# A transformer block with 32 experts: TensorE's order in the expert stage written out, with one pair's combination inside the next pair's products and weight pieces of 8 KB rows

## The chip, the cores and the metric

The kernel runs on one core of a Trainium2 chip. The metric is the time of one execution on the device in microseconds (us). The core has five engines that run their own instruction streams: TensorE (PE, matrix products), VectorE (DVE), ScalarE (ACT), GpSimd (POOL) and SyncE (SP, which here only issues transfers). [...]

## The reference

Two blocks over 512 tokens of width 1024, all in f32. The first: attention and a Fourier mix, then a mixture of 32 experts. The second: an S5 layer, an SSD layer, an MLP behind each. The change lies in the experts and what feeds them:

```python
def hier_moe(h, w_rg, b_rg, w_re, b_re, w_gate, w_up, w_down):
    ...                                   # each token: 2 of 32 experts, and a gate for each
    h_pad = jnp.concatenate([h, jnp.zeros((1, d), h.dtype)], axis=0)
    def expert_block(args):
        tok, wt, e = args
        xb = h_pad[tok]
        y = (jax.nn.silu(xb @ w_gate[e]) * (xb @ w_up[e])) @ w_down[e]
        return y * wt[:, None]
    ...
    return out[:t]                        # the sum of a token's two results

xl = xl + gt2 * hier_moe(h2l.reshape(b * s, d), *moe_args).reshape(b, s, d)
```

`w_gate` and `w_up` are 1024x512 for each expert, `w_down` is 512x1024: 6.3 MB for an expert, 201 MB for all 32.

## The kernel before

`moe` (L916 to L1023) goes over the experts in 8 steps (`st`) of 4 experts, and each step in 2 pairs (`pr`), 16 pairs in all. A pair does, in the order of the code:

- **G, U** (L970): the gate and up products of the two experts, 32 matmuls each, 64 columns of the array for either expert, over 8 pieces of weights. `part` (L922) loads a piece of 1 MiB, 512 rows of one expert, each partition taking 4 rows of 2 KB from four places. Row `k*128 + p` of the weights stands in partition p, so `gather` reads 128 neighbouring columns of `h2h`, `h2l` for its k.
- **gather** (`pg`, L910, L911): for the 4 experts of the next step, the tokens' vectors are picked by products with a one-hot matrix `oh`, 64 matmuls in four PSUM tiles; ScalarE copies them to `xg` (L914). The code has it in each second pair (`pr == 1`) alone.
- **phT** (L982): silu on ScalarE (`sg`), times U on VectorE, then four transposes to `hT`. **pw** (L988): the gate of each slot, eight passes of the array in f32.
- **Y** (L1001): the down product, 32 matmuls over 4 pieces, first all of the left half of the columns, then the right. VectorE scales it (`y`, L1005), ScalarE and VectorE split it into a high and a low part (`yh`, `yl`, L1006, L1007).
- **S5 tables**: `next(self.blocks)` runs one block of `s5_blocks` (L1496 to L1556), which prepares tables of the second block: two transposes `pcd` (L1518), eight VectorE operations on `pb` and `m3` (L1526 to L1538), four transposes `pm2` (L1543), products `pkt` (L1550, L1551), copies `Cd`, `me`, `kt` on ScalarE and three transfers on GpSimd's queue. They use the one PSUM buffer of `psz`.
- **combination**: `pohT` (L1012) transposes the one-hot matrix, and 16 products `pcmb` (L1019, L1020) add the pair's results to the tokens, 8 additions on VectorE (`x`, L1022).

PSUM gives this stage seven buffers, taken in turn by all of these. Nothing orders TensorE's instructions but data, buffers and the scheduler's own choice, so the code's order isn't the order on the engine: in most steps the gather and `pohT` stand inside the products of U and Y. Weights go through a ring of eight buffers of 1 MiB and two of their own (`own`); SP issues a load when TensorE has used up what lay in the buffer.

Ahead of the stage, `pre` computes the tokens' normalised vectors `h2h` (ScalarE, L615) and their remainder `h2l` (VectorE, L620), and in between `router` its choice, with two small operations on ScalarE (L875, L881).

Of the kernel before, what the change touches and what calls it, by code (L numbers as in the profile page):

```python
# [98 lines left out]
class Build:  # L99
    def __init__(self, tc, a, out, ctx, taps=None, mode="all"):  # L100
        self.tc, self.nc, self.a, self.out, self.taps, self.mode = tc, tc.nc, a, out, taps or {}, mode
        self.ctx = ctx
        self.overflow, self.split_eng = True, None
        self.g = self.pool(ctx, "glob", 1)
        self.big = self.pool(ctx, "big", 5)
        self.psz = self.pool(ctx, "psz", 1, space=PSUM)
        self.dr = ctx.enter_context(tc.tile_pool(name="dr", bufs=1, space=DRAM))
# [26 lines left out]
    def split(self, w, shape, pool, name="w", eng=None):  # L134
# [6 lines left out]
        return h, l  # L141

# [245 lines left out]
    def pre(self):  # L388
# [136 lines left out]
        next(self.blocks)  # L525
# [26 lines left out]
        self.sc2, self.sh2 = sc2, sh2  # L552
        nc.vector.scalar_tensor_tensor(sc2, sc2, 1.0, self.col["g_ffn"], op0=ADD, op1=MUL)
        wr, wrs = [late[:, i, 0:288].rearrange("p (k n) -> p k n", k=8) for i in (1, 2)]
# [58 lines left out]

        for t in range(4):
            nc.scalar.activation(self.h2h[:, t], x1[:, t], AF.Copy, scale=rs[:, t:t + 1])  # L615
        with tc.issue_after(self.marks.ins):
            for c in range(2):
                cs = slice(c * 512, c * 512 + 512)
                for t in range(4):
                    nc.vector.scalar_tensor_tensor(self.h2l[:, t, cs], x1[:, t, cs], rs[:, t:t + 1], self.h2h[:, t, cs].bitcast(F32),  # L620
                                                   op0=MUL, op1=SUB)
# [278 lines left out]
    def gather(self, xg, oh2d, n, ks=(0, 8)):  # L900
# [3 lines left out]
        for k0 in range(*ks, per):  # L904
            pt = self.psum((128, per, n), name="pg")
            for i in range(per):
                k = k0 + i
                ks = slice(k * 128, k * 128 + 128)
                for t in range(4):
                    nc.tensor.matmul(pt[:, i], self.h2h[:, t, ks], oh2d[:, t], start=(t == 0), stop=False)  # L910
                    nc.tensor.matmul(pt[:, i], self.h2l[:, t, ks], oh2d[:, t], start=False, stop=(t == 3))  # L911
# [4 lines left out]
    def moe(self):  # L916
# [5 lines left out]
        def part(wt, e, kh, q=None):  # L922
            return self.raw(wt[e, kh * 512:(kh + 1) * 512].rearrange("(k p) n -> p k n", p=128), (128, 4, 512), q=q)
# [6 lines left out]
        down = lambda e, hf: wd[e, :, hf * 512:(hf + 1) * 512].rearrange("(k p) n -> p k n", p=128)  # L930
        xg2 = self.B((128, 2, 2048), name="xg")
        place = lambda w: w.rearrange("p (k n) -> p k n", k=4)

        def part_d(e, hf, w=None):
            if w is None:
                return self.raw(down(e, hf), (128, 4, 512))
# [7 lines left out]
        if self.overflow:  # L944
            self.moe_overflow(xg2[:, 0].rearrange("p (k n) -> p k n", k=4))
        with ExitStack() as cx:
            mp = self.pool(cx, "moe", 2)
            def prepare(st):
# [3 lines left out]

            nxt = prepare(0)
            for st in range(8):
# [4 lines left out]
                for pr in range(2):  # L959
                    eA = e0 + 2 * pr  # L960
                    so = pr * 128
                    G, U = self.psum(name="G"), self.psum(name="U")
                    for w, pt in ((wg, G), (wu, U)):
                        for kh in range(2):
# [3 lines left out]
                            for k in range(4):  # L968
                                for i in range(2):
                                    nc.tensor.matmul(pt[64 * i:64 * i + 64], xg[:, kh * 4 + k, so + 64 * i:so + 64 * i + 64],  # L970
                                                     ws[i][:, k], start=(kh == 0 and k == 0), stop=(kh == 1 and k == 3),
                                                     tile_position=(0, 64 * i), skip_group_check=True)
                    for i in range(4):
                        if pr == 1 and st < 7:
                            self.gather(nxt[1], nxt[0], 256, (2 * i, 2 * i + 2))
                    sg = mp.tile([128, 512], F32, tag="sg", name="sg")
                    hm = sg
                    nc.scalar.activation(sg, G, AF.Silu)
                    nc.vector.tensor_tensor(hm, sg, U, op=MUL)  # L979
                    pt = self.psum(name="phT")  # L980
                    for k in range(4):
                        nc.tensor.transpose(pt[:, k * 128:(k + 1) * 128], hm[:, k * 128:(k + 1) * 128], self.ident)  # L982
                    hT = mp.tile([128, 4, 128], F32, tag="hT", name="hT", bufs=1)
                    nc.scalar.activation(hT, pt.rearrange("p (k s) -> p k s", k=4), AF.Copy)

                    pw = self.psum((128, 4), name="pw")
                    for t in range(4):
                        nc.tensor.matmul(pw, oh2[:, t, so:so + 128].bitcast(F32), self.gw[:, t, e0:e0 + 4],  # L988
                                         start=(t == 0), stop=(t == 3))
                    wv = mp.tile([128, 1], F32, tag="wv", name="wv")  # L990
                    for i in range(2):
                        nc.vector.tensor_copy(wv[64 * i:64 * i + 64], pw[64 * i:64 * i + 64, 2 * pr + i:2 * pr + i + 1])
                    yh = mp.tile([128, 2, 512], F32R, tag="yh", name="yh", bufs=1)
                    yl = mp.tile([128, 2, 512], F32R, tag="yl", name="yl", bufs=1)
                    for hf in range(2):
                        ws = [ahead.pop((id(wd), hf, i)) if eA == 0 and (id(wd), hf, i) in ahead else
                              part_d(eA + i, hf, None if hf else own[i]) for i in range(2)]
                        pt = self.psum(name="Y")
                        for k in range(4):
                            for i in range(2):  # L1000
                                ip = nc.tensor.matmul(pt[64 * i:64 * i + 64], hT[:, k, 64 * i:64 * i + 64], ws[i][:, k],  # L1001
                                                      start=(k == 0), stop=(k == 3), tile_position=(0, 64 * i),
                                                      skip_group_check=True)
                        y = mp.tile([128, 512], F32, tag="y", name="y", bufs=1)
                        nc.vector.scalar_tensor_tensor(y, pt, wv, self.gt2[:, hf * 512:(hf + 1) * 512], op0=MUL, op1=MUL)  # L1005
# [4 lines left out]
                    pt = self.psum(name="pohT")  # L1010
                    for t in range(4):
                        nc.tensor.transpose(pt[:, t * 128:(t + 1) * 128], oh2[:, t, so:so + 128].bitcast(F32), self.ident)  # L1012
                    ohT = mp.tile([128, 512], F32R, tag="ohT", name="ohT", bufs=1)
                    nc.scalar.activation(ohT, pt, AF.Copy)
                    for t in range(4):
                        for hf in range(2):
                            pt = self.psum(name="pcmb")
                            ls = ohT[:, t * 128:(t + 1) * 128]
                            nc.tensor.matmul(pt, ls, yh[:, hf], start=True, stop=False)  # L1019
                            nc.tensor.matmul(pt, ls, yl[:, hf], start=False, stop=True)  # L1020
                            xs = x1[:, t, hf * 512:(hf + 1) * 512]
                            nc.vector.tensor_tensor(xs, xs, pt, op=ADD)  # L1022
# [1020 lines left out]
```

## Time and profile before

| what | us |
|---|---|
| median of 3 runs (2452.0 to 2458.82) | 2454.11 |
| the profiled execution | 2456.05 |
| its span, first to last instruction | 2454.3 |
| expert stage, first gather to last addition | 445.59 to 1063 |
| busy in the span: TensorE | 2281.1 |
| VectorE | 1353.9 |
| ScalarE | 816.7 |

[...] Two warnings for reading: a matmul's duration in a row is longer than the time between two of them, since they overlap, so a pace is read from the starts of two rows; and a TensorE that is shown busy may still be emptying one kind of product before it begins another.

### The profile page before, as it was taken

The page shows a single profiled execution, that of the slowest core. Times are in us where ns is not written, and L with a number is a line of the kernel's source. Part 1 is how long each engine was busy: PE and PEld are TensorE (multiplying, and loading weights), DVE is VectorE, ACT ScalarE, POOL GpSimd, SP SyncE. Part 2 cuts the span into 40 slices and gives each one's busy share as a digit, 9 for nine tenths or more (in the row PEclk, how much of TensorE's full clock was granted, in tenths as well). Part 3 has the DMA queues.
Part 4 walks back from the last instruction along what each step waited for, and adds up shares of the span by engine and source line. Part 5 has one row for each costly group of instructions (what it writes and reads, how often), then busy time and mean ns, then how long its engine had stood idle before and what let it go on. Part 6 is the DMA issues. An engine that isn't in the chain of part 4 may idle for free.

```text
span 2454.3 us, 32253 instructions
## 1 busy us (share of the span) xinstructions
PE 2281.1 (93%) x12503; PEld 1633.9 (67%) x12503; DVE 1353.9 (55%) x2583; ACT 816.7 (33%) x1317; POOL 240.2 (10%) x407
## 2 busy tenths in 40 slices
PE   7988999699998999979999999999999998999997
PEld 4664569344444444368788778787778777888787
DVE  4754445424334242466667884466786778544454
ACT  4232343211111111154333332335654434322332
POOL 0166000011111010000000000000221210000000
PEclk9899999899999999989999999999999999999999
DMA  8577645699999999945545772342332322233330
GB/s 282 163 219 235 196 141 189 248 326 341 355 377 322 331 331 355 340 132 160 175 125 169 228 229 91 95 123 62 112 104 87 111 78 86 69 95 95 94 96 35
DMA packets 327775, 454.02 MB, mean 185 GB/s; under 512 B 22308, under 2 KB 201252, under 8 KB 327620
## 3 DMA queue, kind: packets, MB, share of 16 engines
q1 hardware_dynamic: 318272, 435.23, 53.8%
q0 software_dynamic: 8592, 16.27, 2.1%
q8 instruction: 100, 1.64, 0.3%
q10 hardware_dynamic: 756, 0.43, 0.1%
q14 instruction: 55, 0.45, 0.1%
HBM read 436.14 MB, written 15.73 MB: 184 GB/s over the span
## 4 chain that ended last, share of the span: by engine, by line
PE 54%; DVE 8%; DMA 3%; ACT 3%; issue 2%; POOL 0%; SPq 0%; DVEq 0%; ACTq 0%; POOLq 0%
PE pt L146 13%; PE pt L147 13%; PE pt L148 13%; PE G L970 3%; PE Y L1001 3%; PE U L970 3%; DMA adaw<-in_ada_w 3%; DVE adaacc L314 1%; DVE wl L140 1%; PE pg L910 1%; PE pg L911 1%; PE py L1925 1%; PE pY L1668 0%; DVE x L1327 0%; PE pG L1637 0%
## 5 line engine op out<-in xcount | busy, mean ns | idle before, releaser
L140 DVE TENSOR_TENSOR wl<-w,wh 128x1024 fp32r<-128x1024 f32 (+2 forms) x239 | 287.4, 1207 | 225.1 <-ACT wh L139 221.0
L139 ACT ACTIVATE wh<-w 128x1024 fp32r<-128x1024 f32 (+1 forms) x241 | 249.0, 1040 | 480.5 <-PE pt L147 375.1
L146 PE MATMUL pt<-hh,wh 128*128 128x512 f32 (+2 forms) x976 | 369.0, 383 | 3.2 <-ACT hh L1219 3.0
L147 PE MATMUL pt<-hl,wh 128*128 128x512 f32 (+2 forms) x976 | 367.9, 380 | 0.1
L148 PE MATMUL pt<-hh,wl 128*128 128x512 f32 (+2 forms) x976 | 365.9, 378 | 0.0
L146 PE MATMUL pt<-ab,wh 128*128 128x512 f32 (+1 forms) x576 | 213.4, 375 | 4.8 <-ACT o L1347 2.9
L147 PE MATMUL pt<-ab,wh 128*128 128x512 f32 (+1 forms) x576 | 214.4, 373 | 1.1 <-DVE ab L1296 0.9
L148 PE MATMUL pt<-ab,wl 128*128 128x512 f32 (+1 forms) x576 | 213.7, 372 | 0.0
L146 PEld LDWEIGHTS pt<-hh,wh 128*128 128x128 f32 (+1 forms) x976 | 181.9, 188 | 44.9 <-ACT hh L1219 4.2
L147 PEld LDWEIGHTS pt<-hl,wh 128*128 128x128 f32 (+1 forms) x976 | 182.9, 188 | 39.3 <-issue 3.6
L148 PEld LDWEIGHTS pt<-hh,wl 128*128 128x128 f32 (+1 forms) x976 | 183.0, 188 | 39.0 <-issue 3.5
L1327 DVE SCALAR_TENSOR_TENSOR x<-pt,mod,x 128x512 f32<-128x512 f32 (+1 forms) x184 | 122.3, 678 | 115.2 <-PE pt L148 114.5
L970 PE MATMUL G<-w,xg 128*64 128x512 f32 x512 | 131.8, 602 | 5.3 <-DVE x L1022 5.3
L979 DVE TENSOR_TENSOR sg<-sg,U 128x512 f32<-128x512 f32 x16 | 11.0, 688 | 227.6 <-PE U L970 227.6
L970 PE MATMUL U<-w,xg 128*64 128x512 f32 x512 | 131.1, 594 | 0.0
L146 PEld LDWEIGHTS pt<-ab,wh 128*128 128x128 f32 x576 | 108.2, 190 | 30.2 <-ACT ab L1295 7.6
L147 PEld LDWEIGHTS pt<-ab,wh 128*128 128x128 f32 x576 | 109.4, 190 | 23.3 <-DVE ab L1296 3.5
L148 PEld LDWEIGHTS pt<-ab,wl 128*128 128x128 f32 x576 | 109.3, 190 | 19.9
L1914 POOL TENSOR_TENSOR ec<-ec,BC 128x384 f32<-128x384 f32 x32 | 39.9, 1263 | 686.7 <-PE pt L148 571.3
L970 PEld LDWEIGHTS G<-w,xg 128*64 128x64 f32 x512 | 38.0, 137 | 75.9 <-issue 63.0
L970 PEld LDWEIGHTS U<-w,xg 128*64 128x64 f32 x512 | 40.8, 137 | 70.7 <-issue 69.2
L1022 DVE TENSOR_TENSOR x<-x,pcmb 128x512 f32<-128x512 f32 x128 | 80.5, 673 | 4.7 <-PE pcmb L1020 4.7
(575 smaller groups left out, 4236.5 us busy)
## 6 DMA issues: line engine op xcount, KB each, us to landing
w<-in_w_gate SPq DMA_DIRECT2D x64, 1024.0 KB
w<-in_mlp_w SPq DMA_DIRECT2D x128, 512.0 KB
w<-in_w_up SPq DMA_DIRECT2D x63, 1024.0 KB
extra<-in_w_down SPq DMA_DIRECT2D x32, 1024.0 KB
w<-in_w_down SPq DMA_DIRECT2D x31, 1024.0 KB
adaw<-in_ada_w SPq DMA_DIRECT2D x48, 512.0 KB
adaw<-in_ada_w SPq DMA_DIRECT2D x96, 256.0 KB
w<-in_m_w_in SPq DMA_DIRECT2D x40, 512.0 KB
```

The costliest lines, as they stand in the source:

```text
L139: nc.scalar.activation(h, w, AF.Copy)
L140: (eng or nc.vector).tensor_tensor(l, w, h.bitcast(F32), op=SUB)
L146: nc.tensor.matmul(out, ah, bh, start=start, stop=False, skip_group_check=True)
L147: nc.tensor.matmul(out, ah, bl, start=False, stop=False, skip_group_check=True)
L148: return nc.tensor.matmul(out, al, bh, start=False, stop=stop, skip_group_check=True)
L314: nc.vector.scalar_tensor_tensor(acc, w, ck, acc, op0=MUL, op1=ADD)
L910: nc.tensor.matmul(pt[:, i], self.h2h[:, t, ks], oh2d[:, t], start=(t == 0), stop=False)
L970: nc.tensor.matmul(pt[64 * i:64 * i + 64], xg[:, kh * 4 + k, so + 64 * i:so + 64 * i + 64], ws[i][:, k], start=(kh == 0 and k == 0), stop= ...
L1001: ip = nc.tensor.matmul(pt[64 * i:64 * i + 64], hT[:, k, 64 * i:64 * i + 64], ws[i][:, k], start=(k == 0), stop=(k == 3), tile_position=(0 ...
L1022: nc.vector.tensor_tensor(xs, xs, pt, op=ADD)
L1327: self.nc.vector.scalar_tensor_tensor(xs, src, gate, xs, op0=MUL, op1=ADD)
L1914: nc.gpsimd.tensor_tensor(ec, ec, BC[:, 1, 128:512], op=MUL)
```

## The change

- `pin` chains each TensorE instruction of the stage behind the one before it in the code, so the code's order is the engine's.
- A generator `combine` holds a pair's 16 combination products. The next pair takes a quarter of them after each half of G and of U.
- PSUM's buffers have three tags: two for small things ("a"), three for G, U, Y ("gu"), two for the combination ("c").
- `pohT` comes right behind U, the gather is spread over both pairs of a step (half of a pair's share before `phT`, half behind it), `pw` becomes four products of rounded operands behind the first half of G.
- `s5_blocks` yields three times a block: the loads; `pcd` and the VectorE tables (run at a pair's end); `pm2`, `pkt`, the copies and stores (run before Y of the next pair).
- A weight piece still has 1 MiB, but a partition takes 8 KB in a row: row `p*8 + k` of gate and up, `p*4 + k` of down. So `h2h` and `h2l` are written by k, from every eighth column of `x1`; `hm` reads every fourth column of `sg` and U; and the scale and shift columns take a trip through DRAM (`ssd`, `ssp`). Y goes over both halves of its columns with the first two rows, then with the last two.
- Three tiles that nobody uses (`shift`, `shift2`, `shift3`) move the addresses of others: the big tiles by 96 bytes.

```diff
+    def pin(self, i):
+        if self.pinned:
+            if self.line is not True:
+                self.tc.add_manual_dep(i.ins, self.line.ins.name, mybir.DependencyInfo(
+                    mybir.DependencyClass.NoSync, mybir.DependencyReason.DATA), reason="pin")
+            self.line = i
+        return i
...
+        ssd = self.dr.tile([16, 128], F32, name="ssd")
+        nc.sync.dma_start(ssd, rows)
+        ssp = self.g.tile([128, 2, 8], F32, name="ssp")
+        nc.sync.dma_start(ssp, ssd.rearrange("(c r) (q k) -> (r q) c k", c=2, k=8))
...
-            nc.scalar.activation(self.h2h[:, t], x1[:, t], AF.Copy, scale=rs[:, t:t + 1])
+            nc.scalar.activation(by_k(self.h2h, t, slice(0, 8)), xk(t, slice(0, 8)), AF.Copy, scale=rs[:, t:t + 1])
...
-            return self.raw(wt[e, kh * 512:(kh + 1) * 512].rearrange("(k p) n -> p k n", p=128), (128, 4, 512), q=q)
+            return self.raw(wt[e].rearrange("(p k) n -> p k n", k=8)[:, 4 * kh:4 * kh + 4], (128, 4, 512), q=q)
...
-        down = lambda e, hf: wd[e, :, hf * 512:(hf + 1) * 512].rearrange("(k p) n -> p k n", p=128)
+        down = lambda e, kh: wd[e].rearrange("(p k) n -> p k n", k=4)[:, 2 * kh:2 * kh + 2]
...
+            def combine(ohT, yh, yl):
+                for t in range(4):
+                    for hf in range(2):
+                        pt = self.ps.tile([128, 512], F32, tag="c", name="pcmb")
+                        ls = ohT[:, t * 128:(t + 1) * 128]
+                        pin(nc.tensor.matmul(pt, ls, yh[:, hf], start=True, stop=False))
+                        pin(nc.tensor.matmul(pt, ls, yl[:, hf], start=False, stop=True))
+                        xs = x1[:, t, hf * 512:(hf + 1) * 512]
+                        nc.vector.tensor_tensor(xs, xs, pt, op=ADD)
+                        yield
...
+                    quarters = [(nxt[1], nxt[0], 256, (k, k + 2)) for k in range(0, 8, 2)] if st < 7 else []
+                    quarters = quarters[2 * pr:2 * pr + 2] if st else quarters[:4 * pr]
+                    G, U = gu("G"), gu("U")
...
+                            for _ in range(2):
+                                next(back, None)
...
+                    half = len(quarters) // 2
+                    for q in quarters[:half]:
+                        self.gather(*q)
                     pt = self.psum(name="phT")
...
+                    for q in quarters[half:]:
+                        self.gather(*q)
+                    if eA:
+                        for _ in range(2):
+                            next(self.blocks, None)
...
-                    with tc.issue_after(ia.ins), tc.issue_after(iv.ins), tc.issue_after(ip.ins):
+                    with tc.issue_after(ia.ins), tc.issue_after(iv.ins):
                         next(self.blocks, None)
...
+                    back = combine(ohT, yh, yl)
```

TensorE at the end of a pair without gather, before: the S5 block's `pcd`, the transposed one-hot matrix, the combination, with `pm2` ahead of its last product and `pkt` among the next pair's G.

```order
L1518 MATMUL pcd_4962<-cst_66,cr_4956 64x64 [waits DMASW2_49]
L1012 MATMUL pohT_5000<-cst_66,oh_4333 128x128 x4
L1019 MATMUL pcmb_5007<-yh_4917,ohT_5005 128x512 [waits Activation_49]
L1020 MATMUL pcmb_5007<-yl_4918,ohT_5005 128x512 [waits DVE_49]
...
L1543 MATMUL pm2_4982<-cst_66,pb_4973 128x128 [waits DVE_49,Activation_49]
L1543 MATMUL pm2_4982<-cst_66,pb_4973 128x128 x3
L1019 MATMUL pcmb_5035<-yh_4917,ohT_5005 128x512 [waits DVE_49]
L1020 MATMUL pcmb_5035<-yl_4918,ohT_5005 128x512
L970 MATMUL G_5039<-w_5041,xg_4097 64x512 [waits DMAHW1_49,DVE_49]
L1550 MATMUL pkt_4990<-m3_4974,pb_4973 16x128 [waits DVE_49,Activation_49]
L1550 MATMUL pkt_4990<-m3_4974,pb_4973 16x128 x3
L1551 MATMUL pkt_4990<-dd_4959,cst_66 16x4x16 [waits DMASW1_49]
```

The same engine and place now: Y ends, `pcd` follows, and the next pair's G begins at once.

```order
L1071 MATMUL Y_5222<-w_5235,hT_5169 64x512
L1589 MATMUL pcd_5254<-cst_67,cr_5214 64x64 [waits DMASW3_49,Activation_49]
L1589 MATMUL pcd_5254<-cst_67,cr_5214 64x64 [waits DMASW4_49]
L1022 MATMUL G_5275<-w_5277,xg_4117 64x512 [waits DMAHW7_49]
...
L986 MATMUL pcmb_5289<-yh_5219,ohT_5143 128x512 [waits Activation_49]
L987 MATMUL pcmb_5289<-yl_5220,ohT_5143 128x512 [waits DVE_49]
L986 MATMUL pcmb_5293<-yh_5219,ohT_5143 128x512 [waits Activation_49]
L987 MATMUL pcmb_5293<-yl_5220,ohT_5143 128x512 [waits DVE_49]
L1032 MATMUL pw_5297<-gw2_4355,oh_4813 128x8 x4
L1022 MATMUL G_5275<-w_5305,xg_4117 64x512 [waits DMAHW1_49]
```

The combination has left the pair's end, and its first quarter stands between the halves of the next G, with `pw` behind it. Second place, TensorE between U and Y of a pair, now (15 further `pg` rows behind either row of `pg`):

```order
L987 MATMUL pcmb_5130<-yl_4991,ohT_4914 128x512
L1045 MATMUL pohT_5138<-ident_r_4353,oh_4358 128x128 x4
L933 MATMUL pg_5145<-oh_4813,h2h_4005 128x256 [waits PE_49]
...
L1054 MATMUL phT_5164<-cst_67,hm_5135 128x128 [waits DVE_49,Activation_49]
L1054 MATMUL phT_5164<-cst_67,hm_5135 128x128 x3
L933 MATMUL pg_5171<-oh_4813,h2h_4005 128x256 [waits Activation_49]
...
L1615 MATMUL pm2_5191<-cst_67,pb_5036 128x128 x4
L1622 MATMUL pkt_5199<-m3_5037,pb_5036 16x128 [waits Activation_49]
L1622 MATMUL pkt_5199<-m3_5037,pb_5036 16x128 x3
L1624 MATMUL pkt_5199<-dd_4988,cst_67 16x4x16 [waits DMASW1_49]
L1071 MATMUL Y_5221<-extra_4004,hT_5169 64x512 [waits DMAHW3_49]
```

Here `pohT`, half of the gather, `pm2` and `pkt` have come to stand between U and Y. ScalarE there, now:

```order
L1048 ACTIVATE ohT_5143<-pohT_5138 128x512 [waits PE_49]
L937 ACTIVATE xg_4117<-pg_5145,ssp_3693 128x256 [waits PE_49]
L937 ACTIVATE xg_4117<-pg_5145,ssp_3693 128x256
L1056 ACTIVATE hT_5169<-phT_5164 128x512 [waits DVE_49,PE_49]
L937 ACTIVATE xg_4117<-pg_5171,ssp_3693 128x256 [waits PE_49]
L937 ACTIVATE xg_4117<-pg_5171,ssp_3693 128x256
L1616 ACTIVATE me_5190<-pm2_5191 128x512 [waits DMASW2_49,PE_49]
L1626 ACTIVATE kt_5197<-pkt_5199 16x4x128 [waits DMASW4_49,PE_49]
L1078 ACTIVATE yh_5219<-y_5245 128x512 [waits DVE_49]
```

The copy `me`, which frees the PSUM buffer for `pkt`, now stands behind two copies of the gather.

## Rows read from the trace of the kernel before

**Rows 1.** Busy time by stretch: us of it, each engine, granted clock, DMA share, GB/s.
```profile
602.74:640.00 37.26, 34.13 (x158) 14.23 (x160) 15.59 (x30) 4.55 (x9) 7.07 (x12) 0.95 1.04 361
640.00:1062.90 422.90, 388.20 (x1890) 182.06 (x1890) 149.27 (x284) 72.94 (x142) 54.42 (x89) 0.99 0.94 334
```
**Rows 2.** Waits of TensorE in the expert stage: us in total, times, longest.
```profile
PE pm L1543 <- DVE pb L1538: 14.6, 15, 1.2
PE pcmb L1019 <- ACT ohT L1014: 11.0, 16, 0.7
PE pg L910 <- DVE oh L897: 9.0, 1, 9.0
PE phT L982 <- DVE sg L979: 8.1, 9, 1.2
```
**Rows 3.** TensorE's timeline, pairs' first G: start, us, line and operation, wait.
```profile
486.64 1.70 PE L970 MATMUL G<-w,xg 128*64 128x512 f32 x2 [0.53 <-DVE x L1022]
...
1027.78 1.08 PE L970 MATMUL G<-w,xg 128*64 128x512 f32 x4
```
**Rows 4.** TensorE's timeline in one pair without gather, and Y of a later one.
```profile
529.79 1.05 PE L1550 MATMUL pkt<-m,pb 128*16 128x128 f32 x8
...
545.78 0.66 PE L982 MATMUL phT<-cst,sg 128*128 128x128 f32 x4 [0.85 <-DVE sg L979]
546.27 0.95 PE L988 MATMUL pw<-gw,oh 128*128 128x4 f32 x8
547.18 3.65 PE L1001 MATMUL Y<-extra,hT 128*64 128x512 f32 x16
550.66 3.60 PE L1001 MATMUL Y<-w,hT 128*64 128x512 f32 x16
...
558.71 0.39 PE L1019 MATMUL pcmb<-yh,ohT 128*128 128x512 f32 x1
558.93 0.39 PE L1020 MATMUL pcmb<-yl,ohT 128*128 128x512 f32 x1
...
773.62 5.35 PE L1001 MATMUL Y<-extra,hT 128*64 128x512 f32 x16
```
**Rows 5.** TensorE's timeline where weight products lie between gather products.
```profile
451.27 3.65 PE L970 MATMUL G<-w,xg 128*64 128x512 f32 x16
...
455.08 0.28 PE L911 MATMUL pg<-oh,h2l 128*128 128x256 f32 x1
455.20 0.28 PE L910 MATMUL pg<-oh,h2h 128*128 128x256 f32 x1
...
880.66 3.65 PE L970 MATMUL U<-w,xg 128*64 128x512 f32 x14
...
884.46 0.28 PE L910 MATMUL pg<-oh,h2h 128*128 128x256 f32 x1
```
**Rows 6.** ScalarE's copies of the gather, by line: busy us, mean ns, idle before.
```profile
L914 ACT ACTIVATE xg<-pg,mcol 128x256 f32<-128x256 f32 x64 | 32.6, 559 | 96.3 <-PE pg L911 96.3
```
**Rows 7.** Transfers: two stretches (columns as in Rows 1), and SP's queue, 430 to 1075.
```profile
500.00:515.00 15.00, 14.63 (x102) 10.74 (x100) 1.00 (x3) 4.56 (x9) 0.00 (x0) 1.00 1.05 386
4.00:5.50 1.50, 0.00 (x0) 0.00 (x0) 0.00 (x0) 0.00 (x0) 0.00 (x0) 1.00 1.05 420
...
q1 hardware_dynamic: 103361, 200.10, 87.7%
```
**Rows 8.** Ahead of the stage: the timeline, and a line that reads every eighth column.
```profile
430.01 2.19 ACT L615 ACTIVATE h2h<-x,rqy 128x1024 fp32r<-128x1024 f32 x2 [2.61 <-DVE rqy L212]
...
434.71 0.20 ACT L881 ACTIVATE r_ex<-r_ex 128x4 f32<-128x4 f32 x1 [0.34 <-DVE r_ex L880]
...
438.56 4.05 DVE L620 SCALAR_TENSOR_TENSOR h2l<-x,rqy,h2h 128x512 fp32r<-128x512 f32 x6
...
L1207 ACT ACTIVATE hh<-t x8: 1122/1165/1258, 1075.4 to 1089.0; 128x512 fp32r<-128x512 f32 x8
L1208 DVE TENSOR_TENSOR hl<-t,hh x8: 1099/1138/1182, 1076.5 to 1090.2; 128x512 fp32r<-128x512 f32 x8
```

More of the change, by code (lines that the diff above doesn't have):

```diff
@@ L524, in pre @@
         self.ada_ctx.close()
-        next(self.blocks)
+        for _ in range(4):
+            next(self.blocks)
         late = self.B((128, 4, D), name="late")
@@ new lines, in moe @@
+                            for _ in range(2):
+                                next(back, None)
+                            if (w is wg) and kh == 0:
+                                pw = self.psum((128, 2, 4), name="pw")
+                                for t in range(4):
+                                    pin(nc.tensor.matmul(pw, oh2[:, t, so:so + 128], gw2[:, t, st], start=(t == 0), stop=(t == 3)))
+                                wv = mp.tile([128, 1], F32, tag="wv", name="wv", bufs=4)
+                                for i in range(2):
+                                    ps = slice(64 * i, 64 * i + 64)
+                                    nc.vector.tensor_reduce(wv[ps], pw[ps, :, 2 * pr + i], axis=AX.X, op=ADD)
@@ new lines, in moe @@
+                    sg = mp.tile([128, 512], F32, tag="sg", name="sg", bufs=1)
+                    hm = mp.tile([128, 4, 128], F32, tag="y", name="hm")
+                    k4 = lambda ap: ap.rearrange("s (p k) -> s k p", k=4)
+                    nc.scalar.activation(sg, G, AF.Silu)
+                    nc.vector.tensor_tensor(hm, k4(sg), k4(U), op=MUL)
+                    pt = self.psum(name="pohT")
+                    for t in range(4):
+                        pin(nc.tensor.matmul(pt[:, t * 128:(t + 1) * 128], oh2[:, t, so:so + 128], ident_r, start=True,
+                                             stop=True, skip_group_check=True))
@@ L984, in moe @@
+                    hT = mp.tile([128, 4, 128], F32, tag="sg", name="hT", bufs=1)
                     nc.scalar.activation(hT, pt.rearrange("p (k s) -> p k s", k=4), AF.Copy)
[L986 to L990, printed above, removed]
@@ new lines, in moe @@
+                    Y = [gu("Y") for _ in range(2)]
+                    for kh in range(2):
+                        ws = [ahead.pop((id(wd), kh, i)) if eA == 0 and (id(wd), kh, i) in ahead else
+                              part_d(eA + i, kh, None if kh else own[i]) for i in range(2)]
+                        for hf in range(2):
+                            for k in range(2):
+                                for i in range(2):
+                                    pin(nc.tensor.matmul(Y[hf][64 * i:64 * i + 64], hT[:, 2 * kh + k, 64 * i:64 * i + 64],
+                                                         ws[i][:, k, hf * 512:(hf + 1) * 512], start=(kh == 0 and k == 0),
+                                                         stop=(kh == 1 and k == 1), tile_position=(0, 64 * i),
+                                                         skip_group_check=True))
@@ L1023, in moe @@
+            for _ in back:
+                pass
+            self.line = self.pinned = None
         self.tap("x2pre", x1)
```

125 lines of the change are left out of this document (64 added, 61 removed).

## The prediction

> **What bounds the kernel now.** I read the busy time by stretch first, then TensorE's waits in the expert stage, then its timeline pair by pair, then the transfers. The stage runs from 445.6 to 1063.0, 617.4 us. From the first G of the second pair to that of the last [rows 3] there are 14 pairs in 1027.78 - 486.64 = 541.1 us, so 38.65 us a pair; the first takes 41.0 and the last with its additions 35.2. What a pair's work should take I build from paces. Sixteen weight products go in 550.66 - 547.18 = 3.48 us, so the 96 of a pair in 20.9. The 16 combination products go one in 0.22 [rows 4]: 3.6. Gather products go one in 0.12 [rows 5]; 32 for each pair on average: 3.8. Four transposes take 0.49, `pohT` and `phT` 1.0; `pw` 0.9; `pm2` like the transposes 0.5; `pkt` 1.2 [rows 4]; `pcd` 0.2. That is 32.1 us of the 38.65.
>
> The rest is two things. TensorE stood idle for 422.9 - 388.2 = 34.7 us in the 10.9 pairs from 640 on [rows 1], 3.2 a pair, and the waits name who it waited for: `pm2` for VectorE's table `pb` 15 times, the combination for ScalarE's copy `ohT` 16 times, `phT` for VectorE's product 9 times [rows 2]. The other 3.3 us are shown as busy. Part of them is the change from one kind of product to another: after 16 weight products a second gather product starts 455.08 - 451.27 = 3.81 us after the first of them, of which the products and one gather product explain 3.60; in a later place 14 weight products with one gather product should take 3.17, and took 884.46 - 880.66 = 3.80 [rows 5]. The scheduler mixes gather and weight products piecemeal, so this price is paid often. Part may be weights that come late: one half of Y took 5.2 us from 773.62 on, for 3.48 [rows 4].
>
> Transfers are near their limit but not at it: their share is 0.94 from 640 on, at 334 GB/s, where a saturated stretch shows 1.05 and 386 [rows 1, 7]. A pair moves 334 x 422.9 / 10.94 = 12.9 MB.
>
> **The change, part by part.**
>
> *A pair with gather, in the fixed order.* Weights 20.9, combination 3.6, gather 3.8 (now 32 in each pair), transposes 1.0, `pw` with four passes in place of eight 0.5, `pm2`, `pkt`, `pcd` 1.9: 31.7. Changes of kind: out of G's halves, U's halves and Y, five. The low price is 0.2 on the way out, and I take 0.3 with the way back in; the high one is 0.7 (0.63 by the later place). G's whole half of 16 is the form that the new order has, so 0.3: 1.5 a pair, at most 3.5.
>
> *Waits that stay.* After `pohT` and 16 gather products TensorE does `phT`, then the other 16. With two PSUM buffers of that tag these need the buffer of the first ones, that is both copies `xg` at 0.56 each [rows 6] with some 0.2 for signals, less `phT`'s 0.49: 0.9. Then `pm2` 0.5, and `pkt` needs its one buffer back: `me` stands behind two more `xg` on ScalarE, so 2 x 0.56 + 0.6 + 0.2 - 0.5 = 1.4. Queued behind `pkt` on TensorE is Y, so both are on the path: 2.3.
>
> *Waits that go.* `pb` is made a pair ahead, so `pm2` no longer waits. `ohT` is copied while the gather runs. `phT` has 0.5 + 1.9 us of cover after U for `hm`, which now reads every fourth column; a line on VectorE that reads every eighth takes 1.14 against some 0.7 [rows 8], so it fits with a microsecond to spare. The first combination waits for `yl` of the last pair behind 3.5 us of G; `y`, `yh`, `yl` of the right half are three operations of 512 columns, on VectorE some 0.7 each (`h2l`'s six in 4.05 [rows 8]), with signals about 2.6. An addition frees a combination buffer in 0.7 and has 3.5 until the next quarter. If that cover failed it would cost some 0.5 us a pair.
>
> *Sum of a pair:* 31.7 + 1.5 + 2.3 = 35.5. Twelve pairs are of this kind: 426. The pair with the first gather, worked in the same way, 34.8 (no combination to do, but a whole gather at its start, a part of it at a low clock, and `phT` with less cover); the second has a whole gather of 64, 39.3; the last two have none, 30.7 each. At the end the combination of the last pair is left, set by VectorE's eight additions, 8.2 from Y's end. Together 569.7 for 617.4: **-47.7 us**.
>
> *The layout of 8 KB rows.* `h2h` goes from 1.1 us an operation to about 2.15, by the line that reads every eighth column (1.165 for 512) [rows 8]. `r_ex` of the router stands behind all four on ScalarE and had 0.34 to spare: +3.9. `h2l` follows on VectorE, eight operations that go from 0.74 to 1.14: +3.2. The one-hot matrix and the first gather stand behind, and TensorE idles there (9.0 us for `oh` now [rows 2]): **+7.1 us**, at least 3 if the strided read on this source costs half of that.
>
> *What it gives:* no row shows 8 KB pieces. 2 KB ones (200.10 MB in 103361 packets [rows 7]) saturate at 386, and a stretch where rows of 4 KB come in shows 420 [rows 7]. 12.9 MB take 35.7 us at the 361 of the busiest stage stretch [rows 1], 33.4 at 386, 30.7 at 420. I take 386 or better, so transfers stay behind TensorE's 35.5, except in the last two pairs. From below: nothing bars 8 KB rows from being slower than 2 KB ones, and that is a rival.
>
> *Edits at nothing:* the two small transfers `ssd`, `ssp` stand on SP between loads for the output projection, when TensorE has products loaded for several us; if their cover is gone, +2. The pads move addresses and change no instruction; no row tells a price; I take 0 and allow 6 us either way.
>
> **Sum.** Against the profiled execution 2456.05 - 47.7 + 7.1 = 2415.4. That run was 1.9 above the median of those shown, so 2413.5: **2414 us**.
>
> **Rivals.**
>
> *Changes of kind stay dear.* At 0.7 in place of 0.3, with five a pair, +2.0 us a pair, +30: 2444. For it: the later place in [rows 5], and that TensorE's busy time holds 3.3 us a pair beyond its work. Against: there 14 products stood split, and now the halves are whole.
>
> *Waits and changes hidden.* If the buffers are freed sooner than I count and a change costs what a neighbouring product hides, a pair takes 33.7, and the stage falls by 28 more: 2386. For it: half of the waits is my own sum of signals.
>
> *Transfers set the pace.* At 345 GB/s a pair takes 12.9 / 0.345 = 37.4 us, 16 pairs 598, with 8 for the end and 7 ahead 613: 2450; at 361, 2424. For it: the late Y [rows 4], and loads that wait in SP's queue for a buffer that the end of Y frees. Against: the 386. [...]
>
> *Slower than before:* one mechanism. If 8 KB rows, now 128 in a piece in place of 512, keep fewer of the 16 transfer engines busy at a time, the rate falls. From 12.9 MB in 38.1 us, 339 GB/s, the gain is gone; at 320 a pair takes 40.3, and the time is 2456 + 16 x 40.3 + 8 + 7 - 617 = 2499.
>
> *It doesn't do what it says.* If the missing 3.3 us a pair are late weights and not changes of kind, a fixed order leaves them, pairs stay near 38.5 and the strided reads add 7: about 2460.
>
> **How the numbers follow.** Forecast (with its neighbourhood 2400 to 2428) 0.50; changes dear 0.14; waits hidden 0.14; transfers 0.10; slower 0.06; no gain 0.06. A difference of 0.3%, 7.4 us, is about what a measurement of this kernel can tell from none. Faster by more: the first three and nearly all of the fourth, 0.86; slower by more: 0.08, with a part of the last; the same 0.06. The range takes in the dear changes and the hidden waits: 2386 to 2444.
>
> **What would show it.** In the changed kernel's trace: 35 to 36 us from one pair's first G to the next with gather; waits of `pkt` for `me`, about 1.4, and of the second half of the gather for `xg`, about 0.9, and none of `pm2` for `pb` or the combination for `ohT`; the first gather at about 452.7; a transfer rate above 360 with a share below 1. Pairs of 37.5 with TensorE shown busy would speak for dear changes, with a share of 1.05 for transfers. Pairs at 38.6, or a rate under 340, would make the forecast wrong.

## The result

The changed kernel takes 2384.80 us (median of 4 runs, 2384.53 to 2389.99), against 2453.06 for the kernel before beside it: a ratio of 0.9729, with a 95% interval of 0.9699 to 0.9759. That is 68 us less. The forecast was 2414, 40 us less; the measured time lies 1.2 us below the low end of the range. (Taken by the ratio from the 2454.11 of before that the forecast started from, it is 2387.6, just inside.)

The spans of the two profiled executions differ by 2454.3 - 2383.1 = 71.2 us. Three stretches share that:

| stretch | before | after | difference | forecast |
|---|---|---|---|---|
| start to the first gather of the experts | 445.6 | 451.5 | +5.9 | +7.1 |
| first gather to last addition | 617.4 | 562.9 | -54.5 | -47.7 |
| from there to the end | 1391.3 | 1368.7 | -22.6 | 0, within 6 |

So the stage came out 7 us better than forecast, and three quarters of the miss lie in a stretch to which the prediction gave nothing.

The first stretch also holds work that is nearly the same in every kernel of this case and varies by itself: the first operation on `h2h` starts between 426 and 443 us in the fourteen traces. From that operation to the first gather it is 15.6 us before and 22.4 after, 6.9 more.

### The profile after

The busy time by stretch (us of the stretch, then each engine with its number of instructions, granted clock, DMA share, GB/s), to hold against [rows 1]:

```profile
490.00:700.00 210.00, 198.93 (x1048) 98.12 (x1046) 82.54 (x152) 39.31 (x78) 34.45 (x58) 1.00 0.95 371
700.00:920.00 220.00, 208.97 (x1083) 99.86 (x1080) 94.81 (x178) 41.13 (x83) 39.02 (x66) 1.00 0.96 377
```

TensorE is idle for 430 - 407.9 = 22.1 us in 12.3 pairs, 1.8 a pair, where it was 3.2. The transfers have the same share as before and move a tenth more. TensorE's waits in the stage, to hold against [rows 2]:

```profile
PE pkt L1622 <- ACT me L1616: 16.6, 15, 1.2
PE pg L933 <- DVE oh L920: 12.4, 1, 12.4
PE pg L933 <- ACT xg L937: 8.8, 13, 0.7
PE Y L1071 <- ACT hT L1056: 0.7, 1, 0.7
PE phT L1054 <- DVE hm L1041: 0.7, 1, 0.7
```

`pm2` no longer waits for `pb`, nor the combination for `ohT` or `yh`. The two waits that the prediction said would stay are there, at 1.1 and 0.7 us a pair (forecast 1.4 and 0.9). One pair on TensorE, from the timeline (start, duration, what), to hold against [rows 4]:

```profile
640.62 3.65 PE L1022 MATMUL U<-w,xg 128*64 128x512 f32 x16
644.21 0.50 PE L986 MATMUL pcmb<-yh,ohT 128*128 128x512 f32 x1
644.54 0.39 PE L987 MATMUL pcmb<-yl,ohT 128*128 128x512 f32 x1
...
645.33 3.65 PE L1022 MATMUL U<-w,xg 128*64 128x512 f32 x16
...
655.60 0.60 PE L1615 MATMUL pm<-cst,pb 128*128 128x128 f32 x4
657.36 1.05 PE L1622 MATMUL pkt<-m,pb 128*16 128x128 f32 x8 [1.16 <-ACT me L1616]
...
658.55 3.65 PE L1071 MATMUL Y<-extra,hT 128*64 128x512 f32 x16
662.03 3.60 PE L1071 MATMUL Y<-w,hT 128*64 128x512 f32 x16
665.57 0.30 PE L1589 MATMUL pcd<-cst,cr 64*64 64x64 f32 x2
665.79 3.65 PE L1022 MATMUL G<-w,xg 128*64 128x512 f32 x16
```

Weight products come in whole halves of 16, and Y, `pcd` and the next G stand close together. In the trace the first G of one pair follows that of the last in 34.93 to 35.3 us in the twelve pairs with half of a step's gather (35.5 forecast); before, the 14 pairs of [rows 3] varied from 33.4 to 43.8.

Ahead of the stage, ScalarE and then VectorE, to hold against [rows 8]:

```profile
429.04 4.16 ACT L638 ACTIVATE h2h<-x,rqy 128x1024 fp32r<-128x1024 f32 x2 [2.62 <-DVE rqy L223]
...
437.26 0.20 ACT L904 ACTIVATE r_ex<-r_ex 128x4 f32<-128x4 f32 x1
...
441.85 6.32 DVE L643 SCALAR_TENSOR_TENSOR h2l<-x,rqy,h2h 128x512 fp32r<-128x512 f32 x6
```

`h2h` takes 2.08 us an operation for 1.1, `h2l` 1.05 for 0.68.

And one thing nobody had asked about. In the MLP of the second block, whose code the change doesn't touch, products of 512 columns follow each other like this before:

```profile
2260.16 0.40 PE L146 MATMUL pt<-hh,wh 128*128 128x512 f32 x1
2260.40 0.39 PE L147 MATMUL pt<-hl,wh 128*128 128x512 f32 x1
2260.63 0.40 PE L148 MATMUL pt<-hh,wl 128*128 128x512 f32 x1
2260.86 0.40 PE L146 MATMUL pt<-hh,wh 128*128 128x512 f32 x1
```

and after:

```profile
2192.02 0.39 PE L157 MATMUL pt<-hh,wh 128*128 128x512 f32 x1
2192.25 0.39 PE L158 MATMUL pt<-hl,wh 128*128 128x512 f32 x1
2192.47 0.39 PE L159 MATMUL pt<-hh,wl 128*128 128x512 f32 x1
2192.70 0.39 PE L157 MATMUL pt<-hh,wh 128*128 128x512 f32 x1
```

Three products take 0.70 us before and 0.68 after; the median spacing over all of them is 0.234 and 0.227 us, at the same granted clock of 1.00.

### The profile page after: what moved, and what is told of

It reads as the page before. It is cut to its first block, busy times and chain, and to the rows that moved or that the text cites. A ratio compares the mean times of both kernels' runs of the same rounds, so it can differ in the third digit from the quotient of the medians.

```text
span 2383.1 us, 32055 instructions
## 1 busy us (share of the span) xinstructions
PE 2226.4 (93%) x12440; PEld 1620.5 (68%) x12440; DVE 1362.5 (57%) x2584; ACT 820.9 (34%) x1320; POOL 237.4 (10%) x407
## 4 chain that ended last, share of the span: by engine, by line
PE 62%; DVE 8%; ACT 4%; DMA 3%; issue 3%; POOL 0%; SPq 0%; DVEq 0%; ACTq 0%; POOLq 0%
PE pt L157 12%; PE pt L158 12%; PE pt L159 12%; PE U L1022 5%; PE Y L1071 5%; PE G L1022 5%; DMA adaw<-in_ada_w 2%; PE pcmb L986 2%; PE pg L933 2%; PE pg L934 1%; PE pcmb L987 1%; DVE adaacc L325 1%; DVE wl L142 1%; ACT wh L141 1%; PE pkt L1622 1%
## 5 line engine op out<-in xcount | busy, mean ns | idle before, releaser
L157 PE MATMUL pt<-hh,wh 128*128 128x512 f32 (+2 forms) x976 | 363.4, 377 | 3.2 <-ACT hh L1289 3.0
L158 PE MATMUL pt<-hl,wh 128*128 128x512 f32 (+2 forms) x976 | 362.4, 374 | 0.0
L159 PE MATMUL pt<-hh,wl 128*128 128x512 f32 (+2 forms) x976 | 360.8, 373 | 0.0
L1022 PE MATMUL G<-w,xg 128*64 128x512 f32 x512 | 116.9, 598 | 0.0
L1022 PE MATMUL U<-w,xg 128*64 128x512 f32 x512 | 116.6, 598 | 0.0
L933 PE MATMUL pg<-oh,h2h 128*128 128x256 f32 x256 | 66.0, 295 | 21.2 <-DVE oh L920 12.4
L1022 PEld LDWEIGHTS U<-w,xg 128*64 128x64 f32 x512 | 34.1, 136 | 66.9 <-issue 62.2
```

The source lines that it names most:

```text
L157: nc.tensor.matmul(out, ah, bh, start=start, stop=False, skip_group_check=True)
L158: nc.tensor.matmul(out, ah, bl, start=False, stop=False, skip_group_check=True)
L159: return nc.tensor.matmul(out, al, bh, start=False, stop=stop, skip_group_check=True)
L933: self.pin(nc.tensor.matmul(pt[:, i], self.h2h[:, t, ks], oh2d[:, t], start=(t == 0), stop=False))
L1022: pin(nc.tensor.matmul(pt[64 * i:64 * i + 64], xg[:, kh * 4 + k, so + 64 * i:so + 64 * i + 64], ws[i][:, k], start=(kh == 0 and k == 0), s ...
```

## The experiments

Theories: the order on TensorE sets the stage's pace (the prediction's); rivals: the 8 KB rows set it, or buffers and early tables do and the fixed order little. For the later stages: the unused tiles change the products' pace by their addresses, or something else does.

### The pads

Undone in the changed kernel:

```diff
-        self.g.tile([128, 8], F32, name="shift")
-            self.tp.tile([128, 56], F32, name="shift2", bufs=1)
-        pool.tile([128, 40], F32, name="shift3", bufs=1)
```

> The changed kernel without its three unused tiles. The big tiles then start at 64 modulo 128 bytes, where the changed kernel has 96 and the kernel before 0; the f32 weight halves of the MLPs stay at 96. Theory A (the start of a product's moving operand modulo 64 bytes sets its pace: 0 is slow, 32 is fast): the later stages' products go back from 0.227 us to 0.234, about 2700 of them, +20 us: 2405. Theory B (the operand has to lie at the weights' offset modulo 128): the same here, 2405. Theory C (addresses do nothing, the later stages are faster for another reason): 2385.

Measured: 2401.10 us, ratio 0.9776 (0.9742 to 0.9809), against 0.9729 with the pads: about 12 us, though the two intervals overlap a little. The traces are clearer: up to the end of the stage the two stay within 2 us of each other, then the one without pads loses 15. Behind the stage all ten traces with the pads take 1365 to 1373 us, and this one 1384.

```profile
2204.61 0.40 PE L156 MATMUL pt<-hh,wh 128*128 128x512 f32 x1
2204.84 0.40 PE L157 MATMUL pt<-hl,wh 128*128 128x512 f32 x1
2205.08 0.40 PE L158 MATMUL pt<-hh,wl 128*128 128x512 f32 x1
2205.31 0.40 PE L156 MATMUL pt<-hh,wh 128*128 128x512 f32 x1
```

The spacing is back at 0.233. Alone in the kernel before:

```diff
+        self.g.tile([128, 40], F32, name="shift")
```

> The kernel before with one unused tile of 160 bytes, which puts the big tiles at 32 modulo 128, nothing else changed. Theory A (modulo 64): products at 0.227, the time falls by some 20 us, 2433. Theory B (the weights' offset, 96 modulo 128): no gain, 2453. Theory C: 2453.

Measured: 2444.15 us, ratio 0.9947 (0.9927 to 0.9967), a gain of 13 us; the spacing is 0.229 to 0.231 for most products. And with `[128, 8]` instead:

> The kernel before with one unused tile of 32 bytes, which puts the big tiles at 96 modulo 128, where the changed kernel has them; nothing else changed. Theories A and B: products at 0.227, 2433, so that of the 68 us some 20 belong to the pads alone. Theory C: 2453.

Measured: 2455.29 us, ratio 0.9992 (0.9970 to 1.0015): nothing. The expectation had the place wrong: this tile moves the big tiles by 32 bytes and not by 96, so modulo 128 they lie where the larger tile puts them, and yet one helps and the other doesn't. Theory A, modulo 64, and B, modulo 128, both fall with that. Modulo 256 the five kernels order themselves. The start of the moving operand (`hh`, `hl`, `ab`, and `yh`, which lies elsewhere) in the compiled program, and the median spacing in the trace of that kernel, at a granted clock of 1.00 from 2150 to 2300 in all five:

| start modulo 256 | where | us |
|---|---|---|
| 128 | before (`hh`, `ab`); larger tile alone (`yh`) | 0.234 |
| 160 | small tile alone (`hh`) | 0.233 |
| 192 | changed without pads (`hh`) | 0.233 |
| 224 | changed (`hh`, `yh`); before (`yh`) | 0.227 |
| 0 | small tile alone (`yh`) | 0.233 to 0.234 |
| 32 | larger tile alone (`hh`); changed without pads (`yh`) | 0.229 to 0.231 |

The stationary operands `wh` and `wl` of these stages start at 224 in all five. In the first block they start elsewhere in the kernels built on the one before, and this tells whether the moving operand's place alone counts. With the larger tile alone, moving operands at 32 meet weights at 64 there and weights at 224 in the later stages; thirty products lie between the two starts of each pair of rows:

```profile
43.39 0.40 PE L147 MATMUL pf<-hh,wh 128*128 128x512 f32 x1
...
50.39 0.40 PE L147 MATMUL pf<-hh,wh 128*128 128x512 f32 x1
...
2235.82 0.39 PE L147 MATMUL pt<-hh,wh 128*128 128x512 f32 x1
...
2242.69 0.39 PE L147 MATMUL pt<-hh,wh 128*128 128x512 f32 x1
```

That is 0.233 us a product beside weights at 64 and 0.229 beside weights at 224, at a granted clock of 1.00 in both stretches. So the weights' place goes with the pace too, by 0.004 us. (The transfers that run beside the first stretch, at a share of 1.02, aren't the reason: in the changed kernel, with both operands at 224, the same products take 0.227 beside transfers at 1.09.) Where the two operands start at the same place, 0.227 was measured; where the weights lie 32 bytes behind, as they do in that stage of the first block with moving operands at 32, 128 and 160, 0.233. That the distance between the two sets the pace is the author's estimate from these figures; no run was made to test it.

### The fixed order

```diff
-            self.line = self.pinned = True
```

> The changed kernel without the chain of TensorE's instructions; the scheduler orders them again, and mixes the gather into Y, and the combination and the tables into G, in single products. Theory (the fixed order is the larger part of the stage's gain): more changes of kind and waits, 36.5 to 38.5 us a pair in place of 34.9, 2410 to 2440. Rival (buffers, the halves of the gather and the early tables do it, the chain little): within 10 us of 2385. Rival (8 KB rows are what counts, TensorE waited for weights before): within 10 us of 2385 too.

Measured: 2463.97 us, ratio 1.0021 (1.0002 to 1.0040): the whole gain is gone, and more than the theory asked for. From 640 on a pair takes 41.25 us, longer than before the change. So the 8 KB rows, the buffers and the early tables give no gain when the scheduler chooses the order. What they would bring at the order of before, the run doesn't tell, since the scheduler mixes more here: 125 blocks of weight products in the compiled order, with 122 products that stand without their partner, where the kernel before has 68 and 56. TensorE's timeline shows what the mixing does, the first half of a G:

```profile
726.36 1.07 PE L1021 MATMUL G<-w,xg 128*64 128x512 f32 x2
...
729.30 3.65 PE L1021 MATMUL G<-w,xg 128*64 128x512 f32 x14
732.88 0.50 PE L985 MATMUL pcmb<-yh,ohT 128*128 128x512 f32 x1
```

The 16 products of a half, in one piece 3.59 us from their start to the next kind's, take 1.00 + 3.58 here. The trace has two rows for each f32 product here (x512 on the line of G before, for 256 products of the program), so x2 is a single instruction: the first expert's product without the second's. Otherwise, in the trace of before, the second starts 7 ns behind the first on the other 64 columns, and the four rows of such a couple take 3.48 / 4 = 0.87 us by [rows 4]; the lone product here takes 1.00 up to the next kind's start.

### Lone products or changes of kind?

The two combination steps of each half go inside it, at places that leave the couples whole, as here, or break them, with (1, 0) in place of (0, 1):

```diff
-                            for _ in range(2):
-                                next(back, None)
+                                    if (k, i) in ((0, 1), (2, 1)):
+                                        next(back, None)
```

> The same with the two steps behind the second and the sixth instruction of each half, so that all couples stay whole; as many changes of kind as in the kernel before this one. Theory: 4 more changes of kind a pair at 0.3 us, +1.2 us a pair, about 2403. Rival (each change costs the 0.6 to 0.7 that a place in the trace of before showed): +2.6 a pair, 2424.

> The changed kernel with the two combination steps of each half of G and U put inside that half: one behind the third of its 8 instructions, so that the two experts' products, which otherwise run side by side in the array, come apart, and one behind the sixth. Theory (what the scheduler's mixing cost before was lone products of one expert: one takes as long alone as two together): 4 broken couples a pair at 0.85 to 1.0 us and 4 more changes of kind at 0.3, so 39.5 to 40.2 us a pair, 2453 to 2465. Rival (it is the number of changes between kinds that costs): as the next kernel, 36.1 a pair, 2403.

Measured: whole 2422.01 us (ratio 0.9851, 0.9795 to 0.9907), most pairs at 37.03 us; broken 2473.84 (1.0062, 1.0035 to 1.0090), pairs at 40.42. Four more blocks a pair cost 37.03 - 34.93 = 2.1 us, 0.52 for each, between the theory's 0.3 and its rival's 0.65. Four broken couples cost 3.39 more, 0.85 each, which is the price that was forecast. One half of the broken kind:

```profile
708.68 1.93 PE L1022 MATMUL G<-w,xg 128*64 128x512 f32 x6
710.54 0.50 PE L986 MATMUL pcmb<-yh,ohT 128*128 128x512 f32 x1
710.88 0.40 PE L987 MATMUL pcmb<-yl,ohT 128*128 128x512 f32 x1
711.20 1.93 PE L1022 MATMUL G<-w,xg 128*64 128x512 f32 x6
```

Three instructions (x6) occupy 1.86 us, and two whole couples, four instructions (x8), 1.87 in the kernel that leaves them whole. In the compiled order the stage has 68 blocks of weight products before, 56 of them with an odd number of instructions, and 78 after, none of them odd. Each odd block holds one lone product, half of a broken couple; at half of 0.85 that is an estimate of 24 us for the stage before.

### The rows of the weights

```diff
-            return self.raw(wt[e].rearrange("(p k) n -> p k n", k=8)[:, 4 * kh:4 * kh + 4], (128, 4, 512), q=q)
+            return self.raw(wt[e, kh * 512:(kh + 1) * 512].rearrange("(k p) n -> p k n", p=128), (128, 4, 512), q=q)
-        down = lambda e, kh: wd[e].rearrange("(p k) n -> p k n", k=4)[:, 2 * kh:2 * kh + 2]
+        down = lambda e, kh: wd[e].rearrange("(k p) n -> p k n", p=128)[:, 2 * kh:2 * kh + 2]
```

with `h2h`, `h2l`, `hm` and the columns laid out to match.

> The changed kernel with the weight rows of before (2 KB for gate and up; down in rows of 4 KB, since Y now takes both column halves at once), so without strided reads for the token vectors and without the trip through DRAM; order, PSUM, tables and pads as changed. Theory A (8 KB rows are needed for the pace): the old rows saturate at 361 to 386 GB/s with the table traffic, 12.9 MB take 33.4 to 35.8 us, so pairs rise from 34.9 to about 36, +15 us, less 5 to 6 us for the earlier first gather: about 2394. Rival (transfers had room at the old rows too): pairs stay at 34.9, the first gather comes at about 445, and the time is about 2379.

Measured: 2376.64 us (2371.42 to 2387.87), ratio 0.9660 (0.9616 to 0.9703): the rival holds. Pairs take 34.92 us, not a hundredth more than with 8 KB rows, at the higher share of 1.04:

```profile
640.00:900.00 260.00, 246.46 (x1287) 120.28 (x1287) 102.91 (x193) 47.88 (x96) 41.38 (x71) 1.00 1.04 381
```

And the first gather comes 15.9 us after the first operation on `h2h`, where the changed kernel has 22.4, since nothing is read with a stride: 6.5 us. The medians differ by 8 us and the ratios by 17, with intervals that just overlap, so the trace gives the better price: by itself this part of the change cost some 6.5 us.

### Tables ahead of the gather's second half

The waits that remained can be moved behind each other:

```diff
             nc.scalar.activation(me, pt, AF.Copy)
+            yield
...
+                    if eA:
+                        next(self.blocks, None)
                     for q in quarters[half:]:
                         self.gather(*q)
```

> The changed kernel with the tables' transposes pm2 and their copy me taken ahead of the second half of the gather (a fourth yield in the table generator), so that pkt finds its PSUM buffer free and pm2 covers the gather's wait for its own. Theory (TensorE's order sets the pace): the waits of pkt for me (1.1 us a pair, 16.6 in all) and of the gather for xg (0.7, 8.8 in all) go, 33.2 to 33.4 us a pair, 2361 to 2365. Rival (transfers take over): 12.9 MB at the 370 to 377 GB/s of the stage now are 34.2 to 34.9 us, so at most 10 us fall off, 2375 to 2385.

Measured: 2363.17 us (2361.76 to 2370.95), ratio 0.9622 (0.9577 to 0.9667), the best of all. Pairs take 33.27 us. The waits and the transfers:

```profile
PE pg L933 <- ACT xg L937: 3.1, 13, 0.2
PE pkt L1625 <- ACT me L1618: 1.5, 2, 0.8
```

```profile
640.00:900.00 260.00, 258.09 (x1352) 125.85 (x1350) 113.05 (x210) 51.94 (x104) 47.16 (x80) 1.00 1.01 399
```

TensorE is idle for 1.9 us of 260. The transfers bring 399 GB/s over 260 us, at a share of 1.01. The same with the old rows:

> Two earlier edits together: pm2 and me ahead of the second half of the gather, and the weight rows of before. Theory (rows matter once the pace is higher): the old rows were at a share of 1.04 with 381 GB/s at 34.92 us a pair, which is their limit, so pairs can't follow to 33.27; 12.9 MB / 0.381 = 33.9 us, +0.6 for 13 pairs is +8 against the early tables alone, less about 7 for the earlier first gather: 2360 to 2366. Rival (the rows never matter): pairs at 33.27 and 7 us less ahead of the stage, 2356.

Measured: 2376.22 us, ratio 0.9657 (0.9627 to 0.9688). The first three such pairs take 33.27, the next nine 33.4 to 35.6, 34.05 on average for the twelve:

```profile
640.00:900.00 260.00, 257.63 (x1312) 125.21 (x1312) 102.54 (x193) 49.59 (x99) 42.88 (x73) 1.00 1.04 387
```

Most pairs don't follow to 33.27 here, as the theory said, at 387 GB/s and a share of 1.04. The time is 10 us above its range. Beside the trace with early tables and 8 KB rows the stage is 12.5 us longer, for the 8 that were forecast, and what follows the stage 4.7, which wasn't traced to a part. With 8 KB rows the stage gains twice the 6.5 us that the strided reads cost, so by the traces these rows pay at this pace, which the changed kernel doesn't reach; the intervals of the two ratios still overlap.

### The other parts, undone one by one

The combination at its own pair's end:

```diff
-                    back = combine(ohT, yh, yl)
+                    for _ in combine(ohT, yh, yl):
+                        pass
```

> The changed kernel with each pair's combination at that pair's own end again, in the fixed order. Theory (a pair's combination needs yl and VectorE's additions, which nothing covers at the pair's end): about 2.3 us for yl, eight additions at 0.68 in place of 3.7 of products, and VectorE's table work in their way; less 4 changes of kind at 0.5: 36.8 to 41 us a pair, 2413 to 2475. Rival (whole halves of G and U make up for it): 2385 or less.

Measured: 2507.39 us, ratio 1.0194 (1.0149 to 1.0239), 42 to 44 us a pair, above the range. The waits name the parts:

```profile
PE pcmb L986 <- DVE x L989: 38.3, 31, 2.6
...
PE pcmb L986 <- ACT yh L1078: 11.9, 16, 0.8
PE pcmb L987 <- DVE yl L1079: 4.5, 20, 0.2
```

That is 3.4 us a pair. The mean granted clock is 0.91 from 640 to 900, which by an estimate from the pair's length (9% of 42.6) is 3.8 us more.

A whole block of tables at a pair's end:

```diff
-                    if eA:
-                        for _ in range(2):
-                            next(self.blocks, None)
...
-                        next(self.blocks, None)
+                        for _ in range(3):
+                            next(self.blocks, None)
```

> The changed kernel with a whole block of the S5 tables at each pair's end, in the fixed order. Theory (the three steps keep TensorE from waiting for VectorE): pm2 and pkt then stand right behind pcd, and wait for yl and some 4 to 5 us of table work on VectorE, about 6 us a pair more, less the 1.1 that pkt waits now: 2445 to 2480. Rival (it is only the combination's place that counts): within 15 us of 2385.

Measured: 2513.24 us, ratio 1.0218 (1.0167 to 1.0269), 42.4 to 43.9 us a pair. The wait is the forecast's, 5.7 a pair, but the pair is 8.2 longer on average:

```profile
PE pm L1613 <- DVE pb L1607: 80.0, 14, 5.7
```

```profile
640.00:700.00 60.00, 52.25 (x262) 25.90 (x260) 18.78 (x33) 9.73 (x19) 5.90 (x10) 0.91 0.86 325
```

The granted clock is 0.91 here, for 1.00 in the changed kernel's pairs. The timeline of a later pair shows what goes slower:

```profile
710.70 1.09 PE L1613 MATMUL pm<-cst,pb 128*128 128x128 f32 x4 [5.71 <-DVE pb L1607]
...
714.61 5.74 PE L1022 MATMUL G<-w,xg 128*64 128x512 f32 x16
720.28 0.50 PE L986 MATMUL pcmb<-yh,ohT 128*128 128x512 f32 x1
```

TensorE stood still for 5.7 us, and the clock from 712 to 718 is 0.50: `pkt`, from 712.47 on, takes 1.89 us for the 1.05 of the changed kernel, and the half of G behind it 5.67 from its start to the next kind's, where it takes 3.59 at a clock of 1.00.

The whole gather in the second pair of a step:

```diff
-                    quarters = quarters[2 * pr:2 * pr + 2] if st else quarters[:4 * pr]
+                    quarters = quarters[:4 * pr]
```

> The changed kernel with the whole gather of a step in its second pair, as before, in the fixed order. TensorE's work is the same. Theory A (an even load matters for the transfers): first pairs would take about 30.3 us, for which 12.9 MB need 425 GB/s; with a ring of ten pieces for twelve, one or two us are lost in each step, 2392 to 2400. Rival (the ring evens it out): 2385.

Measured: 2382.84 us, ratio 0.9688 (0.9646 to 0.9729): no difference to the changed kernel. Pairs alternate between 29.75 and 38.8 to 39.7 us, 69.1 on average for two, where it is 69.9. The transfers bring 382 GB/s at a share of 0.97 from 640 to 900, for 380 at 0.97 in the changed kernel, so the ring evens them out, and spreading the gather brought nothing by itself.

The three tags of PSUM's buffers, the place of `pohT` and the four products of `pw` were not taken back alone.

## Why the prediction was wrong in size

**The pads: the term that was off.** "The pads move addresses and change no instruction; no row tells a price; I take 0 and allow 6 us either way." They brought 12 us by the ratios and 15 by the traces of the changed kernel with and without them. There were rows that could have told: in the trace of before, the products with `yh` came at 0.227 and those with `hh` at 0.234, at the same clock and of the same shape. Three with `yh`, to hold against the rows of `hh` above:

```profile
1808.81 0.39 PE L147 MATMUL pt<-yh,wh 128*128 128x512 f32 x1
...
1809.49 0.39 PE L147 MATMUL pt<-yh,wh 128*128 128x512 f32 x1
```

Nobody looked for two paces of one operation. Of the remaining 7 us of the 22.6 behind the stage, addresses can explain some 4, by an estimate: without the pads the operands still moved, from 128 to 192, and the mean spacing went from 0.2343 to 0.2333 over some 4000 products. The rest lies within the 8 us by which the ten traces with pads differ there.

**A gather pair: right in kind.** 34.93 us for 35.5. Most of the difference, 0.5, is in the two waits, 1.8 for 2.3, which the prediction had named with their engines. The 0.2 us for signals that it counted in each is its own estimate, and no run shows it: in the pair above `me` ends on ScalarE at 656.71 + 0.59 = 657.30, and `pkt` starts at 657.36. The twelve such pairs make 6 of the 7 us by which the stage came out better.

**Where the time before went: half right.** The prediction found 3.3 us a pair that were shown as busy and not explained by the work, and put them down to changes of kind, perhaps late weights. The order after has more changes of kind, not fewer (78 blocks for 68); 0.3 for each fits the sum of a pair, and the blocks added in the experiment cost 0.52. What went is the lone products: 56 odd blocks, by estimate some 24 us of the 54.5. The idle time fell by about 1.4 us a pair, some 22 in all, and `pw` by half. The row of 3.80 us in [rows 5], read as a dear change of kind and used for the rival at 2444, had lone products in it. The rival fell for that reason.

**The strided reads: right.** 6.9 us from `h2h` to the first gather for the forecast 7.1; the +5.9 of the table comes from the work ahead, which ran 1 us earlier in this trace. `h2h` was a little cheaper than the line it was estimated from.

**8 KB rows: right that transfers stay behind, and beside the point.** The stage shows 371 to 377 GB/s at a share of 0.95 and 0.96, where the old rows show 1.04 at the same pace. But the old rows keep up at 34.92 us a pair, so this part is a cost of some 6.5 us in this kernel.

**The rivals.** The nearest to the measured time was "waits and changes hidden", 2386, with 0.14; its mechanism didn't happen, since both waits are in the trace. "Slower" and "doesn't do what it says" fell. In the first of these a figure was off: 38.1 us a pair with its 8 and 7 is 7 us slower than before, and the gain is gone at 37.6 already, 343 GB/s.

## What to carry to other kernels

When a scheduler orders products that run side by side on parts of the array, look whether it keeps them together: here a lone one cost as much as two, 0.85 us, and was shown as busy time. Write the order out, with each wait covered by work that is due anyway, and do not expect its parts to help one at a time: here each of three of them, taken back alone, cost the whole gain. If one operation shows two paces in a trace at one clock, as with 0.227 and 0.234 us here, compare the start addresses of its operands, moving and stationary, before anything else.

## What the runs showed of the hardware

- A product of 128x512 took 0.227 to 0.234 us at a granted clock of 1.00, in five kernels that differ in where its operands start. With the weights at 224 modulo 256 bytes it took 0.227 with moving operands at 224, 0.229 to 0.231 at 32 and 0.234 at 128; with moving operands at 32, 0.233 beside weights at 64 for 0.229 beside weights at 224.
- A broken couple of f32 products, 64 columns each, cost 0.85 us more than a whole one, and three products with one of them alone took 1.86 us, for 1.87 of two whole couples.
- Rows of 2 and 4 KB brought 381 GB/s at 34.92 us a pair, and 387 at 34.05, both at a share of 1.04; with 8 KB rows 399 went through at 1.01 and 33.27 us a pair.
- `hm`, which reads every fourth column of a tile in SBUF and of one in PSUM, took 1.07 us where the plain form took 0.69.
- Waits of 3.4 us in sum or 5.7 in one in each pair came with a granted clock of 0.91 and 0.89 from 640 to 900; with the tables at once a pair grew by 8.2 us for a wait of 5.7.
